# A hybrid decoder layer on one core: weights in long runs, and the mixer without GpSimd

## The chip, the cores and the metric

The kernel runs on one core of a Trainium2 chip. The metric is the device time of one execution, in microseconds. The engines are named as in the profile: PE is TensorE (PEld its weight loads), DVE is VectorE, ACT is ScalarE, POOL is GpSimd, SP is SyncE, which issues all the DMAs.

## What is computed

One layer for 256 tokens of width 1024, all in float32 (DEPTH is 1):

```python
c_act = jax.nn.silu(c)
ada = c_act @ w_ada[l] + b_ada[l]
sh_mix, sc_mix, g_mix, sh_ffn, sc_ffn, g_ffn = jnp.split(ada, N_ADA, axis=-1)
h = modulate(rmsnorm(x, norm_mix[l]), sh_mix, sc_mix)
cols = h @ w_in                       # 11520 columns: lru x, lru gate, q, k, v, rwkv, gates
y_a = rglru_branch(lru_x, lru_gate, ...)       # conv, gates, linear scan
y_b = stick_breaking_attention(q, k, v)        # 8 heads
y_c = rwkv7_branch(rw_cols, ...)               # delta-rule state, 16 heads
merged = g_a * (y_a @ p_lru) + g_b * (y_b @ p_sb) + g_c * (y_c @ p_rwkv)
x = x + g_mix[:, None, :] * (merged @ w_out)
h = modulate(rmsnorm(x, norm_moe[l]), sh_ffn, sc_ffn)
x = x + g_ffn[:, None, :] * moe_ffn(h, ...)    # 32 experts, top 4, clamped SwiGLU
return rmsnorm(x, norm_final)
```

## The kernel before

The work has two halves. The mixer (ada, the three branches, their merge, w_out) multiplies activations that lie transposed in SBUF by weights that are streamed in pieces of 256 columns; the MoE streams all 32 experts' weights, 12 MB each, through a ring of 19 tiles of 1 MB.

A **projection** (`proj`) is 256 columns of a weight matrix against all 256 tokens. `load` fetches it in two halves, tiles `raw` of 128 partitions x 4 x 256 (0.52 MB), through a ring of NRAW = 5 tiles. `split_w` makes two float32r tiles of each half: `whi`, a rounded copy made on ACT, and `wlo`, the rest, a subtraction on DVE or, for every `pool`-th half, on GpSimd (PAT, PLRU, PMG: all halves in the lru branch and the first merge, every second one in the second merge, none in attention). The rings of `whi` and `wlo` are NSP = 3 deep. PE then does 48 matmuls per projection, hi x hi, hi x lo and lo x hi. There are 57 projections and four more products of the same size for w_out.

The **ada** columns come in 24 chunks of 256. The eight that the first norm needs are loaded first, in tiles `raw0` of 1.05 MB, and summed on PE (`ada_cols`: eight matmuls of 32 columns against the silu of c, a copy out of PSUM, two matmuls that turn the row into columns). The other sixteen are taken by `ada_next`. In attention, whose four pairs of heads call it three times each, a chunk goes to GpSimd (`ada_cols_g`): two loads into a ring `araw` of its own, a multiplication and sums on GpSimd, and the last two matmuls (`end`) a call later. In the lru branch the other four go through `load` and `ada_cols`.

GpSimd also has the scaling of `qr` (line 418), two steps of the group norm (573, 574), the convolution's first tap (738) and two products of the lru branch (755, 766).

A scheduler of the framework sets the order of each engine's instructions from a cost model; `sooner(n)` raises the priority of a piece, `tc.issue_after` keeps a load from moving ahead. So the branches interleave: the second half of rwkv, with its **triangular solve** (lines 488 to 493, 31 steps of a multiplication and a subtraction on DVE), runs beside the lru branch. On each engine the order is then fixed, and a waiting instruction holds all behind it. SP's queue holds the loads in the order in which ring slots are expected to come free; each waits for the engine that last read the slot.

`x1`, the norm of the MoE and the first 7 expert tiles take the place of rwkv's buffers when these are done; further ring tiles open as the merge, w_out and the splits end. In the MoE each expert is 64 matmuls for gate and up (line 1081), 32 for down (1108) and the scatter (1123); `ew` (879) loads a tile as soon as its slot is free.

Of the kernel before, what the change touches and what calls it, by code (L numbers as in the profile page):

```python
# [80 lines left out]
def trace(tc, pools, I, out, dbg, stop):  # L81
# [139 lines left out]

    def ada_cols_g(pool, nk, col, dst):

        r = mixer.tile([128, 256], F32, name="adarow", tag="adarow", bufs=2)
        for k in range(0, KT, nk):
            raw = pool.tile([128, nk, 256], F32, name="araw", tag="araw", bufs=2)
            with tc.issue_after(last[0].ins):
                SY.dma_start(raw, ada_src(col)[:, k:k + nk])
            G.tensor_tensor(raw, raw, bcast(csil[:, k:k + nk], 2, 256), ALU.mult)  # L229
            if nk == 4:  # L230
                G.tensor_tensor(raw[:, 0:2], raw[:, 0:2], raw[:, 2:4], ALU.add)
            if k == 0:
                G.tensor_tensor(r, raw[:, 0], raw[:, 1], ALU.add)
            else:
                G.tensor_tensor(r, r, raw[:, 0], ALU.add)
                G.tensor_tensor(r, r, raw[:, 1], ALU.add)

        def end():
            ps = ptp([128, 2], "adacol")
            for i in range(2):  # L240
                T.matmul(ps[:, i:i + 1], r[:, i * 128:i * 128 + 128], onesq[:, 0:1], start=True, stop=True)
            V.tensor_tensor(dst, ps, P("b_ada", col // 128, 2), ALU.add)

        return end
# [1101 lines left out]
```

## Time and profile before

| | |
|---|---|
| median of 3 runs | 1581.53 us (1578.42 to 1583.39) |
| the profiled execution | 1581.08 us, its span 1579.4 us |
| busy in the span | PE 92%, DVE 43%, ACT 25%, POOL 17% |
| DMA | 498.84 MB, 167350 packets; 99921 of them under 2 KB |
| expert weights | 384 loads of 1 MB, all on SP's queue |

The page gives busy time by engine over the whole span; the stretches differ so much that the rows by window say more. A matmul's duration on the page includes its pipeline, so PE's busy share is no measure of how near it is to its peak. A wait is put down to what ended it.

### The profile page before, as it was taken

How to read it: one execution, taken by the hardware profiler on the slowest of the kernel's cores; microseconds unless marked ns; L12 is line 12 of the kernel's file. 1: busy time of each engine (PE TensorE's matmuls, PEld its weight loads, DVE VectorE, ACT ScalarE, POOL GpSimd, SP SyncE). 2: the span in 40 equal slices, each digit the busy share in tenths (PEclk: the TensorE clock that was granted, in tenths of full speed). 3: DMA queues.
4: the chain of work that ended last, by engine and by line, in shares of the span. 5: the costliest groups of instructions: out<-in, count | busy, mean ns of one | idle time of the engine just before them, and what ended most of it. 6: DMA issues, size and time to landing. Idle time of an engine off the chain costs nothing. (4 is left out here: it accounts for less than half of the span.)

```text
span 1579.4 us, 20890 instructions
## 1 busy us (share of the span) xinstructions
PE 1459.9 (92%) x8416; PEld 833.8 (53%) x8416; DVE 686.6 (43%) x1284; ACT 397.1 (25%) x692; POOL 264.5 (17%) x213
## 2 busy tenths in 40 slices
PE   6999799987999998999999889999989989989897
PEld 4889799876899997334333223333323223223233
DVE  5698945889628655222313113313213212212323
ACT  4634333754735443101101001001001001101101
POOL 0184673655544100000000000000000000000000
PEclk7979879988999998999999999999999999999999
DMA  9655543343335968899999999999999999999995
GB/s 324 202 184 162 159 155 101 116 138 111 113 118 155 317 227 321 351 418 417 418 416 418 417 416 416 418 416 417 417 418 415 418 418 415 418 418 416 417 419 204
DMA packets 167350, 498.84 MB, mean 316 GB/s; under 512 B 12625, under 2 KB 99921, under 8 KB 134481
## 3 DMA queue, kind: packets, MB, share of 16 engines
q1 hardware_dynamic: 167248, 497.46, 81.9%
q8 instruction: 68, 1.11, 0.3%
q14 instruction: 34, 0.27, 0.0%
HBM read 496.37 MB, written 1.05 MB: 315 GB/s over the span
## 5 line engine op out<-in xcount | busy, mean ns | idle before, releaser
L1081 PE MATMUL pg<-ew,xe 128*64 128x512 f32 x1024 | 273.7, 612 | 29.0 <-DMA ew<-in_w_gu_dram 28.7
L1081 PE MATMUL pu<-ew,xe 128*64 128x512 f32 x1024 | 264.2, 597 | 0.0
L1108 PE MATMUL pd<-ew,act 128*64 128x512 f32 x992 | 230.4, 601 | 22.8 <-ACT act L1100 22.8
L174 PE MATMUL mm<-hhi,whi 128*128 128x256 f32 x720 | 216.0, 300 | 6.5 <-ACT whi L153 6.5
L174 PE MATMUL mm<-hhi,wlo 128*128 128x256 f32 x720 | 215.6, 300 | 3.3 <-DVE wlo L156 2.8
L174 PE MATMUL mm<-hlo,whi 128*128 128x256 f32 x720 | 216.0, 300 | 0.0
L1081 PEld LDWEIGHTS pg<-ew,xe 128*64 128x64 f32 x1024 | 68.3, 138 | 179.8 <-issue 103.9
L153 ACT ACTIVATE whi<-raw 128x1024 fp32r<-128x1024 f32 x122 | 128.8, 1058 | 123.8 <-PE mm L174 98.8
L174 PEld LDWEIGHTS mm<-hhi,whi 128*128 128x128 f32 x720 | 146.3, 203 | 10.5 <-ACT whi L153 6.7
L1081 PEld LDWEIGHTS pu<-ew,xe 128*64 128x64 f32 x1024 | 74.6, 138 | 146.2 <-issue 146.2
L174 PEld LDWEIGHTS mm<-hhi,wlo 128*128 128x128 f32 x720 | 146.4, 204 | 8.2 <-issue 3.4
L1108 PEld LDWEIGHTS pd<-ew,act 128*64 128x64 f32 x992 | 69.4, 138 | 151.9 <-issue 115.1
L174 PEld LDWEIGHTS mm<-hlo,whi 128*128 128x128 f32 x720 | 146.8, 204 | 5.3 <-issue 4.7
L1114 DVE TENSOR_TENSOR yd<-pd,gff 128x512 f32<-128x512 f32 x31 | 21.5, 692 | 269.2 <-PE pd L1108 244.6
L156 DVE TENSOR_TENSOR wlo<-raw,whi 128x1024 fp32r<-128x1024 f32 x82 | 112.4, 1373 | 51.1 <-ACT whi L153 50.7
L156 POOL TENSOR_TENSOR wlo<-raw,whi 128x1024 fp32r<-128x1024 f32 x40 | 98.7, 2469 | 95.5 <-ACT whi L153 93.5
L1123 PE MATMUL pc<-yd,swt 64*128 64x512 f32 x248 | 96.0, 628 | 0.0
L1125 DVE TENSOR_TENSOR x<-x,pc 128x512 f32<-128x512 f32 x124 | 84.1, 680 | 11.6 <-PE pc L1123 10.7
L1123 PEld LDWEIGHTS pc<-yd,swt 64*128 64x128 f32 x248 | 30.0, 185 | 49.8 <-issue 28.5
L229 POOL TENSOR_TENSOR araw<-araw,csil 128x1024 f32<-128x1024 f32 x24 | 51.0, 2129 | 31.3 <-DMA araw<-in_w_ada_dram 31.3
L1053 ACT ACTIVATE xe<-xps,adaf,A 128x256 f32<-128x256 f32 x32 | 18.1, 565 | 100.4 <-DVE xe L1052 100.1
L1100 ACT ACTIVATE act<-act_ps 128x256 f32<-128x256 f32 x64 | 24.5, 383 | 72.8 <-PE act_ps L1098 71.4
(820 smaller groups left out, 1878.6 us busy)
## 6 DMA issues: line engine op xcount, KB each, us to landing
ew<-in_w_gu_dram SPq DMA_DIRECT2D x256, 1024.0 KB, 20.0
ew<-in_w_down_dram SPq DMA_DIRECT2D x128, 1024.0 KB, 20.0
raw<-in_w_in_dram SPq DMA_DIRECT2D x90, 512.0 KB, 4.3
araw<-in_w_ada_dram SPq DMA_DIRECT2D x24, 512.0 KB, 4.9
raw<-in_w_ada_dram SPq DMA_DIRECT2D x8, 1024.0 KB, 12.4
raw<-in_w_ada_dram SPq DMA_DIRECT2D x8, 512.0 KB, 3.6
raw<-in_p_sb_dram SPq DMA_DIRECT2D x8, 512.0 KB, 3.5
raw<-in_p_lru_dram SPq DMA_DIRECT2D x8, 512.0 KB, 3.5
```

What stands on the lines that cost most here:

```text
L153: A.activation(hi, src, AF.Copy)
L156: eng.tensor_tensor(lo, src, r32(hi), ALU.subtract)
L174: T.matmul(ps[:, c], w[i][:, k, c * 128:c * 128 + 128], x[j][:, q * 4 + k], start=(q + c + k + n == 0), stop=(q == 1 and k == 3 and n == 2 ...
L229: G.tensor_tensor(raw, raw, bcast(csil[:, k:k + nk], 2, 256), ALU.mult)
L1053: A.activation(xe[:, k + 1, 0:n], xps[:, 1, 0:n], AF.Identity, scale=A2[:, k + 1:k + 2], bias=sh2[:, k + 1:k + 2])
L1081: i = T.matmul(p[hf * 64:hf * 64 + 64], xe[:, k], gu[k][:, c0:c0 + 512], start=False, stop=(k == KT - 1), skip_group_check=True)
L1100: A.activation(at, tp, AF.Copy)
L1108: i = T.matmul(pd[hf * 64:hf * 64 + 64], at[:, k % 2, (k // 4) * 64:(k // 4) * 64 + 64], w[:, hf * 512:hf * 512 + 512], start=(n == 0), st ...
L1114: V.tensor_tensor(yd, pd, gff2, ALU.mult)
L1123: T.matmul(ps, swt[sl, t], yd[sl], start=True, stop=True)
L1125: V.tensor_tensor(y[:, t, csl], y[:, t, csl], ps, ALU.add)
```

## The change

The host lays the weights out by pieces. w_ada, w_in, the three branch projections and w_out become arrays [piece of 256 columns, half, partition, 1024], so that a half is one run of 4 KB per partition instead of four of 1 KB; w_down's tiles get one run of 8 KB per partition instead of two of 4 KB (w_gu had such runs). The rwkv up-projections and the b_gu rows are stacked so that one load replaces two and four. Bytes and matmuls stay as they were.

In the mixer GpSimd keeps memsets and masks alone. All low parts go to DVE; the twelve ada chunks of attention go through `load` and `ada_cols` on PE, and the sixteen late chunks leave PSUM on ACT instead of DVE; the two products of the lru branch and the second centring go to DVE; the scaling of `qr`, the squares and the first tap go to ACT. NRAW becomes 7, and the ring `araw` goes.

```diff
-    NRAW, NSP = 5, 3
+    NRAW, NSP = 7, 3
     def ada_src(col):
-        return I["w_ada"].rearrange("(k p) n -> p k n", p=128)[:, :, col:col + 256]
+        return I["w_ada"][col // 256].rearrange("q p n -> p q n")
     def load(src, col):
-        v = src.rearrange("(k p) n -> p k n", p=128)
         for q in range(2):
             t = wraw.tile([128, 4, 256], F32, name="raw", tag="raw", bufs=NRAW)
-            last[0] = SY.dma_start(t, v[:, q * 4:q * 4 + 4, col:col + 256])
+            last[0] = SY.dma_start(t.rearrange("p k n -> p (k n)"), src[col // 256, q])
-    PAT, PLRU, PMG = 0, 1, (1,2,0)
-    def split_w(src, pool=None):
+    def split_w(src):
         A.activation(hi, src, AF.Copy)
-        nsplit[0] += 1
-        eng = G if pool and nsplit[0] % pool == 0 else V
-        eng.tensor_tensor(lo, src, r32(hi), ALU.subtract)
+        V.tensor_tensor(lo, src, r32(hi), ALU.subtract)
-    def ada_cols(raw, col, dst, pspace=ptp):
+    def ada_cols(raw, col, dst, pspace=ptp, late=False):
-        V.tensor_copy(r, ps)
+        if late:
+            A.activation(r, ps, AF.Copy)
+        else:
+            V.tensor_copy(r, ps)
-    def ada_cols_g(pool, nk, col, dst):
...
-            SY.dma_start(raw, ada_src(j * 256))
+            SY.dma_start(raw.rearrange("p (q k) n -> p q (k n)", q=2), ada_src(j * 256))
-        SY.dma_start(upw[0:64], I["rw_w_up"][:, b * 512:b * 512 + 512])
-        SY.dma_start(upw[64:128], I["rw_a_up"][:, b * 512:b * 512 + 512])
+        SY.dma_start(upw, I["rw_up"][b])
-                G.tensor_scalar(qr[:, cl, :, 0:64], ch(kx), P("rw_k_k", ct), None, ALU.mult)
+                A.activation(qr[:, cl, :, 0:64], ch(kx), AF.Copy, scale=P("rw_k_k", ct))
-            (G if t else V).tensor_tensor(yv[:, t], yv[:, t], bcast(mean[:, t], 2, 64), ALU.subtract)
-            G.tensor_tensor(sq[:, t], yv[:, t], yv[:, t], ALU.mult)
+            V.tensor_tensor(yv[:, t], yv[:, t], bcast(mean[:, t], 2, 64), ALU.subtract)
+            A.activation(sq[:, t], yv[:, t], AF.Square)
-    def ada_next(pool=None, nk=4):
-        if ends:
-            ends.pop(0)()
+    def ada_next():
...
-        if pool:
-            ends.append(ada_cols_g(pool, nk, 2048 + i * 256, dst[:, 2 * j:2 * j + 2]))
-        else:
-            ada_cols(load(I["w_ada"], 2048 + i * 256), 2048 + i * 256, dst[:, 2 * j:2 * j + 2])
+        ada_cols(load(I["w_ada"], 2048 + i * 256), 2048 + i * 256, dst[:, 2 * j:2 * j + 2], late=True)
-            G.tensor_scalar(xc, xr[:, cc], P("conv_w", ct), P("conv_b", ct), ALU.mult, ALU.add)
+            A.activation(xc, xr[:, cc], AF.Identity, scale=P("conv_w", ct), bias=P("conv_b", ct))
-        G.tensor_tensor(gt, gq, gt, ALU.mult)
+        V.tensor_tensor(gt, gq, gt, ALU.mult)
-            G.tensor_tensor(ix, s8, ix, ALU.mult)
+            V.tensor_tensor(ix, s8, ix, ALU.mult)
-            for i in range(4):
-                SY.dma_start(raw[i * 32:i * 32 + 32], I["b_gu"][:, j * D + i // 2 * 512:j * D + i // 2 * 512 + 512])
+            SY.dma_start(raw, I["b_gu2"][j])
-    dsrc = I["w_down"].rearrange("e (q k p) n -> e q p k n", p=128, k=2)
+    dsrc = I["w_down"].rearrange("e q p (k n) -> e q p k n", k=2)
+def pieces(w, n, parts):
+    rows, cols = w.shape
+    v = w.reshape(parts, rows // parts // 128, 128, cols // n, n).transpose(3, 0, 2, 1, 4)
+    return np.ascontiguousarray(v).reshape(cols // n, parts, 128, -1)
```

The scheduler makes a new order of this. Three places matter here. Names of tiles carry numbers that differ between the programs.

SP's queue where attention begins, before: halves of w_in go into `raw`, halves of ada chunks into `araw`.

```order
L142 DMA raw_1477<-in_w_in_dram 128x4x256
L142 DMA raw_1479<-in_w_in_dram 128x4x256
L228 DMA araw_1482<-in_w_ada_dram 128x4x256
L228 DMA araw_1487<-in_w_ada_dram 128x4x256
L142 DMA raw_1552<-in_w_in_dram 128x4x256
L142 DMA raw_1554<-in_w_in_dram 128x4x256
L142 DMA raw_1631<-in_w_in_dram 128x4x256
L228 DMA araw_1561<-in_w_ada_dram 128x4x256
```

The same queue after the change, from the second pair's V to the third pair's V, with the engines whose progress each load waits for (DMAHW stands for an earlier DMA, DVE for a split, PE for an ada chunk's matmuls):

```order
L142 DMA raw_2092<-in_w_in_dram 128x1024 [waits DMAHW1_49,DVE_49]
L142 DMA raw_2094<-in_w_in_dram 128x1024 [waits DMAHW4_49,DVE_49]
L142 DMA raw_2096<-in_w_ada_dram 128x1024 [waits DMAHW6_49,DMAHW5_49,DVE_49]
L142 DMA raw_2098<-in_w_ada_dram 128x1024 [waits DMAHW7_49,PE_49]
L142 DMA raw_2174<-in_w_in_dram 128x1024 [waits PE_49]
L142 DMA raw_2176<-in_w_in_dram 128x1024 [waits PE_49]
L142 DMA raw_2178<-in_w_ada_dram 128x1024 [waits DMAHW2_49,PE_49]
L142 DMA raw_2180<-in_w_ada_dram 128x1024 [waits DMAHW3_49,PE_49]
L142 DMA raw_2256<-in_w_in_dram 128x1024 [waits PE_49]
L142 DMA raw_2258<-in_w_in_dram 128x1024 [waits DMAHW0_49,DVE_49]
```

Ada halves now alternate with w_in halves in one ring; the first two rows are the third pair's Q, `raw_2174` and `raw_2176` its K.

PE at that place after the change: the end of the third pair's Q (mm_2116), three ada chunks, and the first matmul of its K (mm_2198).

```order
L194 MATMUL adaps_1792<-raw_1790,crep_92 32x256 x4
L168 MATMUL mm_2116<-hhi_134,wlo_2146 128x256
L168 MATMUL mm_2116<-hhi_134,whi_2145 128x256
L168 MATMUL mm_2116<-hlo_135,whi_2145 128x256
L168 MATMUL mm_2116<-hhi_134,wlo_2146 128x256
L202 MATMUL adacol_1803<-quad_94,adarow_1801 128x1 x2
L194 MATMUL adaps_1874<-raw_1870,crep_92 32x256 x4
L194 MATMUL adaps_1874<-raw_1872,crep_92 32x256 x4
L202 MATMUL adacol_1885<-quad_94,adarow_1883 128x1 x2
L194 MATMUL adaps_1956<-raw_1952,crep_92 32x256 x4
L194 MATMUL adaps_1956<-raw_1954,crep_92 32x256 x4
L168 MATMUL mm_2198<-hhi_134,whi_2199 128x256
```

Before, only the two matmuls of an `adacol` stood here, since GpSimd had made the sums. The three chunks belong to the second pair, and hold their slots up to here.

DVE at the beginning of the second triangular solve, before (`subt` and `xb` are the solve):

```order
L492 TENSOR_TENSOR subt<-lb,xb 128x30
L493 TENSOR_TENSOR xb<-xb,subt 128x30
L492 TENSOR_TENSOR subt<-lb,xb 128x58
L493 TENSOR_TENSOR xb<-xb,subt 128x29x2
L492 TENSOR_TENSOR subt<-lb,xb 128x56
L493 TENSOR_TENSOR xb<-xb,subt 128x28x2
```

And after the change:

```order
L150 TENSOR_TENSOR wlo<-raw,whi 128x1024
L464 TENSOR_TENSOR subt<-lb,xb 128x30
L203 TENSOR_TENSOR adag<-adacol,pc 128x2
L465 TENSOR_TENSOR xb<-xb,subt 128x30
L464 TENSOR_TENSOR subt<-lb,xb 128x58
L465 TENSOR_TENSOR xb<-xb,subt 128x29x2
L727 SCALAR_TENSOR_TENSOR s_3927<-bb,s_3927 128x512
L464 TENSOR_TENSOR subt<-lb,xb 128x56
L465 TENSOR_TENSOR xb<-xb,subt 128x28x2
L150 TENSOR_TENSOR wlo<-raw,whi 128x1024
```

Before, no low part stands inside this solve on DVE, since the lru branch's are on GpSimd; now sixteen and more do. On PE the matmuls that follow the solve (line 505, now 477) stand after 34.2 projections before, and after 39.1 now.

## Rows read from the trace of the kernel before

**Rows 1.** The page: busy time, share of the span and instructions of each engine.

```profile
PE 1459.9 (92%) x8416; PEld 833.8 (53%) x8416; DVE 686.6 (43%) x1284; ACT 397.1 (25%) x692; POOL 264.5 (17%) x213
```

**Rows 2.** Busy us by stretch: length, engines (instructions), granted clock, DMA share, GB/s.

```profile
0.00:52.00 52.00, 38.24 (x290) 28.18 (x291) 27.15 (x85) 24.53 (x37) 4.25 (x32) 0.80 0.99 304
52.00:110.00 58.00, 55.45 (x367) 47.49 (x365) 46.33 (x63) 32.88 (x53) 32.74 (x23) 0.91 0.61 192
110.00:300.00 190.00, 178.97 (x1419) 167.34 (x1420) 141.53 (x226) 78.84 (x122) 107.32 (x94) 0.88 0.45 137
300.00:420.00 120.00, 102.41 (x850) 89.35 (x850) 109.85 (x186) 67.82 (x99) 69.42 (x41) 0.87 0.44 133
420.00:500.00 80.00, 79.37 (x663) 74.96 (x661) 36.62 (x44) 41.29 (x55) 39.41 (x18) 0.98 0.37 109
500.00:600.00 100.00, 97.90 (x784) 93.43 (x785) 66.43 (x91) 45.96 (x67) 11.37 (x6) 1.00 0.80 269
...
660.00:1558.00 898.00, 842.31 (x3666) 293.65 (x3663) 228.39 (x512) 86.21 (x214) 0.00 (x0) 0.98 1.02 416
```

**Rows 3.** PE's longest wait between 660 and 1560: total us, times, longest.

```profile
PE pg L1081 <- DMA ew<-in_w_gu_dram: 28.7, 39, 4.2
```

**Rows 4.** Windows: 4 KB runs of w_down, 8 KB of w_gu, 1 KB of w_ada.

```profile
1308.00:1312.00 4.00, 4.00 (x17) 1.38 (x17) 2.57 (x7) 0.42 (x1) 0.00 (x0) 1.00 1.03 410
1320.00:1326.00 6.00, 5.16 (x27) 2.08 (x26) 1.17 (x2) 1.54 (x4) 0.00 (x0) 1.00 1.01 422
8.00:34.00 26.00, 20.24 (x169) 10.71 (x169) 12.32 (x48) 7.71 (x15) 0.00 (x0) 0.75 1.09 348
```

**Rows 5.** POOL's timeline from 360 us: start, duration, line, operands.

```profile
361.84 2.53 POOL L156 TENSOR_TENSOR wlo<-raw,whi 128x1024 fp32r<-128x1024 f32 x1 [2.75 <-ACT whi L153]
366.39 2.45 POOL L156 TENSOR_TENSOR wlo<-raw,whi 128x1024 fp32r<-128x1024 f32 x1 [2.03 <-ACT whi L153]
```

**Rows 6.** DVE's timeline in the same stretch.

```profile
360.76 0.42 DVE L747 TENSOR_TENSOR ix<-ix,xc 128x256 f32<-128x256 f32 x1
...
362.03 2.61 DVE L747 TENSOR_TENSOR ix<-ix,xc 128x256 f32<-128x256 f32 x1
...
366.64 2.35 DVE L493 TENSOR_TENSOR xb<-xb,subt 128x126 f32<-128x126 f32 x1
...
369.83 0.28 DVE L493 TENSOR_TENSOR xb<-xb,subt 128x120 f32<-128x120 f32 x1
```

**Rows 7.** DVE's groups by form, 300 to 420: busy us, mean ns, idle before.

```profile
L740 DVE SCALAR_TENSOR_TENSOR xc<-xr,pc,xc 128x254 f32<-128x254 f32 x8 | 9.8, 1243 | 0.0
L740 DVE SCALAR_TENSOR_TENSOR xc<-xr,pc,xc 128x255 f32<-128x255 f32 x8 | 8.1, 1026 | 0.0
...
L740 DVE SCALAR_TENSOR_TENSOR xc<-xr,pc,xc 128x253 f32<-128x253 f32 x8 | 3.6, 469 | 0.0
```

**Rows 8.** DVE's groups in 560 to 600, where POOL is idle.

```profile
L156 DVE TENSOR_TENSOR wlo<-raw,whi 128x1024 fp32r<-128x1024 f32 x14 | 17.0, 1222 | 9.7 <-ACT whi L153 9.7
```

**Rows 9.** PE's timeline, 0 to 50: two ada chunks, at full clock and at half.

```profile
15.97 1.07 PE L200 MATMUL adaps<-raw,crep 128*32 128x256 f32 x16
...
21.74 1.93 PE L200 MATMUL adaps<-raw,crep 128*32 128x256 f32 x16 [0.79 <-DMA raw<-in_w_ada_dram]
```

**Rows 10.** Waits of SP's queue, 52 to 500: total us, times, longest.

```profile
SPq L142 <- POOL wlo L156: 137.4, 31, 9.5
...
SPq L228 <- POOL adarow L233: 26.5, 5, 6.9
```

**Rows 11.** DMA issues by line: count, size, median us from issue to landing.

```profile
raw<-in_p_sb_dram SPq DMA_DIRECT2D x8, 512.0 KB, 3.5
```

**Rows 12.** The page's costliest groups: ACT's high parts.

```profile
L153 ACT ACTIVATE whi<-raw 128x1024 fp32r<-128x1024 f32 x122 | 128.8, 1058 | 123.8 <-PE mm L174 98.8
```

**Rows 13.** Tile wlo in 300 to 500: durations min/median/max, first and last start.

```profile
L156 POOL TENSOR_TENSOR wlo<-raw,whi x34: 2349/2402/2773, 301.6 to 497.3; 128x1024 fp32r<-128x1024 f32 x34
```

More of the change, by code (lines that the diff above doesn't have):

```diff
@@ L164, in pmm, with proj @@
         return psum.tile([128, 512], F32, name=name, tag="mm", bufs=3)
-    def proj(raw, x, pool=None):
+    def proj(raw, x):
         ps = pmm().rearrange("p (c t) -> p c t", c=2)
         for q in range(2):
-            w = split_w(raw[q], pool)
+            w = split_w(raw[q])
             for c in range(2):
@@ L220, in ada_cols_v @@
         V.tensor_tensor(dst, ps, P("b_ada", col // 128, 2), ALU.add)
-    def ada_cols_g(pool, nk, col, dst):
[L224 to L233, printed above, removed]
-            else:
[L235 to L244, printed above, removed]
     def diag2(t, cols):
@@ L370, in rwkv_half @@
         upw = rw.tile([128, 512], F32, name="upw")
-        SY.dma_start(upw[0:64], I["rw_w_up"][:, b * 512:b * 512 + 512])
-        SY.dma_start(upw[64:128], I["rw_a_up"][:, b * 512:b * 512 + 512])
+        SY.dma_start(upw, I["rw_up"][b])
         gup = rw.tile([128, 512], F32, name="gup")
-        SY.dma_start(gup, I["rw_g_up"][:, b * 512:b * 512 + 512])
+        SY.dma_start(gup, I["rw_g_up"][b])
         qr = rw.tile([128, 4, 4, 128], F32, name="qr")
@@ L616, in trace @@
     later = list(range(16))
-    ends = []
-    def ada_next(pool=None, nk=4):
-        if ends:
-            ends.pop(0)()
+    def ada_next():
         if not later:
@@ L626, in ada_next @@
         dst, j = ((adag, i) if i < 4 else (adaf, i - 4) if i < 12 else (adag, i - 8))
-        if pool:
-            ends.append(ada_cols_g(pool, nk, 2048 + i * 256, dst[:, 2 * j:2 * j + 2]))
-        else:
-            ada_cols(load(I["w_ada"], 2048 + i * 256), 2048 + i * 256, dst[:, 2 * j:2 * j + 2])
+        ada_cols(load(I["w_ada"], 2048 + i * 256), 2048 + i * 256, dst[:, 2 * j:2 * j + 2], late=True)
     ap = pools("attn", bufs=1)
@@ L689, in attention_pair @@
             if ADA[pr][i]:
-                ada_next(ap)
+                ada_next()
             t = a2("qkv")
-            ps = proj(raw, h2, PAT)
+            ps = proj(raw, h2)
             A.activation(t, ps, AF.Copy, scale=128.0 ** -0.5 if i == 0 else 1.0)
@@ L724, in lru_pair @@
         raw_x, raw_g = load(w_in, OFF_LX + b * 256), load(w_in, OFF_LG + b * 256)
-        if ends:
-            ends.pop(0)()
         if ADAL[b]:
@@ L729, in lru_pair @@
         xr = l2("xr")
-        A.activation(xr, proj(raw_x, h2, PLRU), AF.Copy)
+        A.activation(xr, proj(raw_x, h2), AF.Copy)
         for cc in range(2):
@@ L747, in lru_pair @@
             V.tensor_tensor(ix[:, cc], ix[:, cc], xc, ALU.mult)
-        ps = proj(raw_g, h2, PLRU)
+        ps = proj(raw_g, h2)
         gq = g2("gq")
@@ L915, in trace @@
             sg = g2("gsig")
-            A.activation(sg, proj(raw_g, h2, PMG[br]), AF.Sigmoid)
-            ps = proj(raw_p, yhl, PMG[br])
+            A.activation(sg, proj(raw_g, h2), AF.Sigmoid)
+            ps = proj(raw_p, yhl)
             if br == 0:
@@ L1319, in trace, with halves @@
         finish(gain(ew_tile()[:, 0:D]))
+def pieces(w, n, parts):
+    rows, cols = w.shape
+    v = w.reshape(parts, rows // parts // 128, 128, cols // n, n).transpose(3, 0, 2, 1, 4)
+    return np.ascontiguousarray(v).reshape(cols // n, parts, 128, -1)
+def halves(w):
+    return np.ascontiguousarray(w.reshape(w.shape[0], 2, -1).transpose(1, 0, 2))
 def layout(x, c, w_ada, b_ada, norm_mix, norm_moe, norm_final, w_in, conv_w, conv_b,
@@ L1328, in layout @@
     res = {"x": a["x"][0], "pc": np.ascontiguousarray(pc), "b_router": a["b_router"]}
-    for n in ("w_ada", "w_in", "rw_w_up", "rw_a_up", "rw_g_up", "p_lru", "p_sb", "p_rwkv",
-              "w_out", "w_router", "w_gu", "b_gu", "w_down", "b_down"):
+    for n in ("p_lru", "p_sb", "p_rwkv", "w_out", "w_in", "w_ada"):
+        res[n] = pieces(a[n][0], 256, 2)
+    res["w_down"] = np.ascontiguousarray(a["w_down"][0].reshape(NE, 4, 2, 128, D).transpose(0, 1, 3, 2, 4)).reshape(NE, 4, 128, 2 * D)
+    for n in ("w_router", "w_gu", "b_gu", "b_down"):
         res[n] = a[n][0]
+    res["rw_up"] = halves(np.concatenate([a["rw_w_up"][0], a["rw_a_up"][0]]))
+    res["rw_g_up"] = halves(a["rw_g_up"][0])
+    b = a["b_gu"][0].reshape(NE, 2, 2, 512).transpose(1, 2, 0, 3)
+    res["b_gu2"] = np.ascontiguousarray(np.stack([b, b], axis=2)).reshape(2, 128, 512)
     res["lru_w"] = np.stack([a["lru_wa"][0], a["lru_wx"][0]], axis=2)
```

1 line of the change is left out of this document (removed).

## The prediction

> **What bounds the kernel now.** I read first the page's busy line [rows 1], then the span cut into stretches [rows 2], then the waits inside a stretch. The profiled execution took 1581.08 us, 1579.4 of it span; the median of the runs shown is 1581.53, so the sum below, made against 1581.08, can be read against either. A measurement of this kernel can tell about 0.3%, 4.7 us, from no change.
>
> Rows 2 show two kernels in one. From 660 us to 1558 us the DMA share is 1.02 at 416 GB/s: the expert weights stream without a pause, and TensorE, 842.3 us busy of 898, waits for them [rows 3]. What counts there is bytes per us, and when the stream gets going. Before that, the mixer is no single engine's. In 300 to 420 VectorE is busy 109.9 of 120 us while TensorE is idle for 17.6, with a granted clock of 0.87; in 110 to 300 TensorE is idle for 11.0 us, at 0.88; from 420 on TensorE is nearly full at a clock of 0.98 to 1.00. The DMA share of 0.37 to 0.61 between 52 and 500 says that bandwidth is not what the mixer lacks.
>
> Part of VectorE's busy time is not work. At 361.84 GpSimd starts a low part of 2.53 us [rows 5]; a VectorE multiplication of two SBUF tiles that takes 0.42 us at 360.76 takes 2.61 at 362.03, and ends as GpSimd ends. The same happens to the triangular solve at 366.64 (2.35 instead of 0.28) [rows 6]. The convolution taps with 253 columns take 469 ns and the same taps with 254 columns 1243 [rows 7]: (1243 - 469) x 8 = 6.2 us, and (1026 - 469) x 8 = 4.5 us, lost in two groups alone. SyncE pays too: it stands 137.4 us for GpSimd's low parts and 26.5 us for its ada sums, with weight loads queued behind [rows 10].
>
> **The change, term by term.**
>
> *Long runs at the start.* The eight ada chunks of 1.049 MB come in 1 KB runs at 348 GB/s in 8 to 34 us; in the stream, 4 KB runs move at 410 [rows 4]. 8.39 MB take 24.1 us at the one and 20.5 at the other: **-3.6 us**, on the path, because the first projection waits for the last chunk. The single load of the small rw and b_gu tables instead of two and four only shortens SyncE's queue; nothing is counted.
>
> *Long runs in the stream.* The gate-up weights already come in 8 KB runs; w_down goes from 4 KB to 8 KB: 410 against 422 GB/s [rows 4]. 898 us at 416 GB/s are 373.6 MB, a third of it w_down: 124.5 MB take 303.7 us or 295.1: **-8.6 us**. Between nothing and this lies the range; I take the end, as TensorE has 56 us of room in the stretch [rows 2].
> The Trainium skill speaks against both terms: "DMA: Bandwidth & Descriptors", Specifications, puts line rate at transfers of 512 B and more, so 1 KB runs would already be enough, and gives 358 GB/s as HBM's limit for a core. By that both terms would be 0. The trace disagrees on both: 348, 410 and 422 by length, and 416 sustained.
>
> *Ada on TensorE.* Twelve chunks move from GpSimd. A chunk's eight matmuls take 1.07 us at full clock and 1.93 at half [rows 9]: 12 x 1.07 = **+12.8 us** (23.2 at half clock) in 110 to 300, where TensorE is 94% busy. Their sums to columns were on TensorE before. Sixteen copies out of PSUM, eight scalings, eight convolution starts and four squares go to ScalarE; none can exceed the 1.058 us of a split four to eight times as wide [rows 12], so 38 us at the very most, and ScalarE has 25 to 112 us free in each of these stretches [rows 2]: nothing.
>
> *The ring that ada now shares.* This is the term of the order rows. Twelve chunks now take slots of the seven-slot ring, two each, and TensorE works off three in a row at a pair's end. SyncE's rows show what follows: the two halves of the next K weights wait for PE, that is for the chunk's matmuls. Each then needs its turn behind one other half (0.52 MB at 410: 1.3 us), a landing of 3.5 us [rows 11], and a split of 1.06 on ScalarE and 1.22 on VectorE [rows 8, 12]: 7.1 us. TensorE has two more chunks, their columns and four matmuls meanwhile, some 3.2 us. So 3.9 us of waiting; I charge it at two of the four groups, **+7.8 us**. The lower end is 0 (loads early enough), the upper is the first rival.
>
> *VectorE without GpSimd.* In 52 to 110 TensorE loses 2.6 us idle and 0.09 x 58 = 5.2 to the clock; in 110 to 300, 11.0 and 0.12 x 190 = 22.8; in 300 to 500, 18.2 and 0.13 x 120 + 0.02 x 80 = 17.2 [rows 2]. I expect the idle time back, and half of the clock's, since the clock fell where the engine had been waiting: **-5.2, -22.4 and -26.8 us**. Ends: nothing, and all of it.
> Against that, VectorE takes over 34 low parts between 300 and 500 [rows 13], 34 x 1.222 = 41.5 us [rows 8], and eight products of 512 columns, between 0.42 and 1.22 us each, say 0.7: 47 us. What it gets back there lies between 10.7 us (the two groups above) and GpSimd's whole 108.8 us [rows 2]; I take 40. VectorE ends 7 us longer in a stretch where it is nearly full: **+7 us**. The order rows show that the second solve now stretches over split after split, so part of that lands where VectorE had 43 us free, in 420 to 500.
>
> From 500 to 660 and in the last 21 us I expect nothing: TensorE is 98% busy there, or the code is the same.
>
> Sum: -3.6 - 8.6 + 12.8 + 7.8 - 5.2 - 22.4 - 26.8 + 7 = -39.0 us; 1581.1 - 39 = **1542 us**. By the start and the stream alone, nothing would remain after the ada matmuls are paid.
>
> **The rivals.**
>
> *The shared ring starves TensorE (slower).* Three held chunks are six of seven slots. If all twelve chunks make TensorE wait for a load and a split, 7.1 us less one chunk's own 1.07 each, that is 12 x 6.0 = 72 us in place of 7.8: 1542 - 7.8 + 72 = 1606. It decides from (39.0 + 7.8) / 12 = 3.9 us per chunk. For it: the order rows name PE in SyncE's waits six times in a row. Against it: splits run up to three halves ahead (NSP), and TensorE has a projection's remaining matmuls to work on wherever a group does not stand right at a projection's end. 9%.
>
> *The stalls are hidden anyway (no change).* TensorE counts 94% busy in 110 to 300. If VectorE's lost time only fills gaps that other waits would leave, the start and the stream bring 12.2 us and the ada matmuls cost 12.8: 1582. For it: in 110 to 300 TensorE is idle for only 6% of the time. Against it: GpSimd's blocking falls in the solve, which everything behind it in the rwkv branch needs. 7%.
>
> *Everything comes back (faster still).* All idle time and all lost clock of 52 to 500, 31.8 + 45.2 us, plus 12.2, less 12.8: 1581.1 - 76.4 = 1505. 20%.
>
> *Runs of 1 KB are long enough already.* Then 12.2 us fall away: 1554. The page named above would have it so. The rates of rows 4 contradict it, though they stand beside other differences of place: 4%.
>
> **The numbers.** The forecast has 60%. Faster by more than 0.3% (under 1577) are the forecast, the third and the fourth rival and a little of the second: 0.85. Within 0.3%: most of the second, 0.05. Slower: the first and the rest of the second, 0.10. The range runs from 1508, close to the third rival, to 1577; outside lie the first rival, most of the second and some of the third, about 2 in 10.
>
> **What would show it.** Right: no VectorE product over 1 us in the solve; DMA near 400 GB/s in the first 30 us, and the first projection 3 to 4 us sooner; 420 GB/s in the stream, its last byte about 39 us sooner; the second solve longer than before on the clock, with TensorE busy throughout. Wrong: TensorE gaps of 4 us and more after each group of three ada chunks; a stretch of 300 to 500 no shorter, with VectorE full; a stream that TensorE bounds, its DMA share under 1.

## The result and the profile after

The changed kernel takes 1555.92 us (median of 4 runs, 1551.51 to 1559.59) against 1580.68 of before in the same comparison: a ratio of 0.9841, 95% interval 0.9809 to 0.9873. It is faster, by 24.8 us where 39 were forecast. A second comparison gave 1554.19 and 0.9852 (0.9821 to 0.9883). The profiled execution took 1559.59 us, 1557.8 of it span: 21.6 less than the profiled one of before.

The page's busy line, in the columns of [rows 1]:

```profile
PE 1455.1 (93%) x8608; PEld 830.7 (53%) x8608; DVE 643.3 (41%) x1330; ACT 413.3 (27%) x728; POOL 11.0 (1%) x59
```

GpSimd has 11.0 us of work left for 264.5, and VectorE is 43 us less busy though it has 40 low parts more. The span by stretch, in the columns of [rows 2]:

```profile
0.00:52.00 52.00, 39.89 (x322) 30.20 (x323) 30.49 (x92) 28.81 (x45) 4.25 (x32) 0.90 0.88 341
52.00:110.00 58.00, 58.00 (x463) 49.32 (x462) 41.13 (x73) 34.50 (x55) 1.41 (x4) 1.00 0.52 170
110.00:300.00 190.00, 179.03 (x1465) 159.82 (x1465) 107.63 (x216) 80.76 (x129) 2.31 (x18) 0.89 0.42 141
300.00:420.00 120.00, 110.29 (x877) 101.70 (x877) 105.02 (x218) 89.86 (x134) 1.20 (x3) 0.94 0.47 155
420.00:500.00 80.00, 80.00 (x753) 75.32 (x752) 38.57 (x45) 29.09 (x40) 0.00 (x0) 0.96 0.34 110
500.00:600.00 100.00, 99.78 (x807) 95.15 (x805) 69.07 (x112) 48.71 (x78) 1.80 (x2) 1.00 0.78 297
660.00:1534.00 874.00, 820.39 (x3593) 287.52 (x3590) 223.12 (x500) 84.99 (x211) 0.00 (x0) 0.99 1.01 420
```

The row to look at is 110 to 300: VectorE is 34 us less busy there, and yet TensorE is idle for 11.0 us and at 0.89 of its clock, as before (11.0 and 0.88). 52 to 110 is now full at full clock.

The mixer from its first projection matmul to the last one of w_out, before and after (same columns):

```profile
34.72:612.69 577.97, 544.07 (x4298) 501.90 (x4299) 418.38 (x640) 280.50 (x415) 263.25 (x201) 0.92 0.54 171
```

```profile
30.99:597.66 566.67, 545.99 (x4491) 499.12 (x4492) 374.57 (x686) 296.28 (x451) 9.74 (x47) 0.94 0.51 175
```

So it begins 3.7 us sooner and is 11.3 us shorter. One profile says this only to some us: in the profiled execution of the second comparison (run after_again, the same kernel) the mixer is 5 us shorter again, and its stretch of 110 to 300 has as much idle time (10.7 us) at a clock of 0.92 for 0.89:

```profile
30.49:592.20 561.71, 539.03 (x4489) 493.08 (x4490) 374.95 (x686) 296.00 (x451) 10.69 (x47) 0.95 0.51 177
110.00:300.00 190.00, 179.28 (x1507) 160.57 (x1504) 111.72 (x225) 84.94 (x137) 2.31 (x18) 0.92 0.43 144
```

The rates, in the windows of [rows 4] (w_down, w_gu, the first ada chunks):

```profile
1308.00:1312.00 4.00, 4.00 (x22) 1.29 (x18) 0.00 (x0) 0.00 (x0) 0.00 (x0) 1.00 1.01 420
1320.00:1326.00 6.00, 5.47 (x23) 1.96 (x22) 4.57 (x11) 1.19 (x3) 0.00 (x0) 1.00 1.02 423
8.00:34.00 26.00, 21.89 (x186) 13.66 (x187) 15.92 (x54) 10.05 (x17) 0.00 (x0) 0.83 1.03 409
```

(The first two windows stand at places of the stream; all its runs are 8 KB now.) The stream moves 420 GB/s where it moved 416, the start 409 where it moved 348.

VectorE's groups in 300 to 420, which answer to [rows 7], and the multiplications of both triangular solves (tile `subt`: shortest, median and longest ns, first and last start):

```profile
L150 DVE TENSOR_TENSOR wlo<-raw,whi 128x1024 fp32r<-128x1024 f32 x28 | 34.2, 1221 | 4.9 <-ACT whi L149 4.6
...
L703 DVE SCALAR_TENSOR_TENSOR xc<-xr,pc,xc 128x255 f32<-128x255 f32 x8 | 3.8, 480 | 0.0
L703 DVE SCALAR_TENSOR_TENSOR xc<-xr,pc,xc 128x254 f32<-128x254 f32 x8 | 3.7, 478 | 0.0
L703 DVE SCALAR_TENSOR_TENSOR xc<-xr,pc,xc 128x253 f32<-128x253 f32 x8 | 3.7, 479 | 0.0
...
L464 DVE TENSOR_TENSOR subt<-lb,xb x62: 176/263/301, 126.5 to 418.3; 128x126 f32<-128x126 f32 x6, 128x30 f32<-128x30 f32 x4, 128x56 f32<-128x56 f32 x4, 128x78 f32<-128x78 f32 x4
```

The taps of 1243 and 1026 ns are all 480 now, and no multiplication of the solve takes over 0.301 us, where before the longest took 2.358. The stalls of VectorE beside GpSimd, the mechanism behind [rows 5, 6], are gone. The Trainium skill ("SBUF — State Buffer", SBUF: two separate sides) says that an operation of VectorE with two SBUF inputs and one of GpSimd that reads SBUF take a shared pair of ports for a whole instruction in turn. The trace of before agrees: in [rows 5, 6] the two long operations of VectorE end 0.27 and 0.15 us after the low parts of GpSimd beside which they started.

What TensorE waits for in 110 to 420, before and after, the longest lines of each list (total us, times, longest):

```profile
PE mm L174 <- ACT whi L153: 6.5, 1, 6.5
PE tp L744 <- issue: 5.7, 1, 5.7
PE tp L675 <- DVE beta L672: 4.8, 2, 3.2
PE tp L744 <- DVE xc L740: 2.9, 1, 2.9
PE mm L174 <- DVE wlo L156: 2.8, 2, 1.7
```

```profile
PE mm L168 <- ACT gsig L878: 6.7, 1, 6.7
PE ssq L389 <- ACT k_sq L388: 4.3, 1, 4.3
PE mm L168 <- ACT gq L714: 3.0, 1, 3.0
PE mm L168 <- ACT whi L149: 2.4, 2, 1.6
```

By the whole lists VectorE ended 11.7 us of these waits before and 2.6 after, ScalarE 8.8 before and 18.1 after: ScalarE has taken VectorE's place. Its timeline before the longest of these waits ends (start, duration):

```profile
398.35 1.06 ACT L149 ACTIVATE whi<-raw 128x1024 fp32r<-128x1024 f32 x1
399.43 1.28 ACT L722 ACT_TABLE_LOAD   x1
400.72 0.63 ACT L722 ACTIVATE aa<-s 128x512 f32<-128x512 f32 x1
401.38 0.63 ACT L723 ACTIVATE s<-s 128x512 f32<-128x512 f32 x1
401.92 0.61 ACT L726 ACTIVATE bb<-aa 128x512 f32<-128x512 f32 x1
402.55 1.28 ACT L878 ACT_TABLE_LOAD   x1
403.85 0.60 ACT L878 ACTIVATE gsig<-mm 128x512 f32<-128x512 f32 x1
```

TensorE needs the PSUM tile that the sigmoid of line 878 is to empty, and the sigmoid stands behind the lru branch's last steps and two table loads.

### The profile page after: what moved, and what is told of

Same layout as the page of the kernel before. It is cut to its first block, busy times and chain, and to the rows that moved or that the text cites. A ratio compares the mean times of both kernels' runs of the same rounds, so it can differ in the third digit from the quotient of the medians.

```text
span 1557.8 us, 21164 instructions
## 1 busy us (share of the span) xinstructions
PE 1455.1 (93%) x8608; PEld 830.7 (53%) x8608; DVE 643.3 (41%) x1330; ACT 413.3 (27%) x728; POOL 11.0 (1%) x59
## 5 line engine op out<-in xcount | busy, mean ns | idle before, releaser
L1043 PE MATMUL pg<-ew,xe 128*64 128x512 f32 x1024 | 269.4, 603 | 25.2 <-DMA ew<-in_w_gu_dram 25.2
L168 PE MATMUL mm<-hhi,whi 128*128 128x256 f32 x720 | 212.6, 295 | 5.7 <-ACT gq L714 3.0
L168 PE MATMUL mm<-hhi,wlo 128*128 128x256 f32 x720 | 211.2, 293 | 1.1 <-DVE wlo L150 1.1
L168 PE MATMUL mm<-hlo,whi 128*128 128x256 f32 x720 | 211.7, 294 | 0.0
L150 DVE TENSOR_TENSOR wlo<-raw,whi 128x1024 fp32r<-128x1024 f32 x122 | 148.9, 1223 | 96.4 <-ACT whi L149 95.3
L168 PEld LDWEIGHTS mm<-hhi,whi 128*128 128x128 f32 x720 | 142.5, 198 | 12.8 <-issue 3.8
L168 PEld LDWEIGHTS mm<-hhi,wlo 128*128 128x128 f32 x720 | 142.2, 197 | 7.8 <-issue 5.2
L168 PEld LDWEIGHTS mm<-hlo,whi 128*128 128x128 f32 x720 | 142.3, 198 | 5.6 <-issue 4.8
L1076 DVE TENSOR_TENSOR yd<-pd,gff 128x512 f32<-128x512 f32 x31 | 21.5, 692 | 270.8 <-PE pd L1070 246.2
L1087 DVE TENSOR_TENSOR x<-x,pc 128x512 f32<-128x512 f32 x124 | 84.4, 683 | 11.7 <-PE pc L1085 10.7
L1015 ACT ACTIVATE xe<-xps,adaf,A 128x256 f32<-128x256 f32 x32 | 18.1, 565 | 101.3 <-DVE xe L1014 101.0
L194 PE MATMUL adaps<-raw,crep 128*32 128x256 f32 x384 | 30.3, 433 | 9.9 <-DVE spt L579 9.1
L1014 DVE TENSOR_SCALAR xe<-xps,A,adaf 128x256 f32<-128x256 f32 x32 | 17.4, 544 | 44.4 <-PE xps L1011 44.4
## 6 DMA issues: line engine op xcount, KB each, us to landing
ew<-in_w_gu_dram SPq DMA_DIRECT2D x256, 1024.0 KB, 19.8
ew<-in_w_down_dram SPq DMA_DIRECT2D x128, 1024.0 KB, 19.8
```

The costliest lines, as they stand in the source:

```text
L150: V.tensor_tensor(lo, src, r32(hi), ALU.subtract)
L168: T.matmul(ps[:, c], w[i][:, k, c * 128:c * 128 + 128], x[j][:, q * 4 + k], start=(q + c + k + n == 0), stop=(q == 1 and k == 3 and n == 2 ...
L194: T.matmul(ps[32 * j:32 * j + 32], crep[:, q * 4 + j, :], raw[q][:, j], start=(q == 0), stop=(q == 1))
L1014: V.tensor_scalar(xe[:, k, 0:n], xps[:, 0, 0:n], A2[:, k:k + 1], sh2[:, k:k + 1], ALU.mult, ALU.add)
L1015: A.activation(xe[:, k + 1, 0:n], xps[:, 1, 0:n], AF.Identity, scale=A2[:, k + 1:k + 2], bias=sh2[:, k + 1:k + 2])
L1043: i = T.matmul(p[hf * 64:hf * 64 + 64], xe[:, k], gu[k][:, c0:c0 + 512], start=False, stop=(k == KT - 1), skip_group_check=True)
```

## The experiments

All times in one table. Five comparisons stand behind it: the changed kernel's first; runs_only to low_gpsimd; the changed kernel's second with no_ada, own_ring and mix_c; ada_load to ring_eight; and ada_late. The kernel before had medians of 1576.89 to 1580.99 in them, so across comparisons the ratios compare best (0.001 is 1.6 us).

| kernel | median us | ratio to before | 95% interval |
|---|---|---|---|
| changed kernel, first and second time | 1555.92, 1554.19 | 0.9841, 0.9852 | 0.9809-0.9873, 0.9821-0.9883 |
| runs_only | 1564.15 | 0.9911 | 0.9879-0.9942 |
| mixer_only | 1572.83 | 0.9971 | 0.9954-0.9988 |
| ada_gpsimd | 1559.42 | 0.9875 | 0.9843-0.9908 |
| low_gpsimd | 1572.20 | 0.9976 | 0.9946-1.0006 |
| no_ada | 1524.94 | 0.9666 | 0.9650-0.9682 |
| own_ring | 1556.65 | 0.9865 | 0.9848-0.9881 |
| mix_c | 1556.96 | 0.9868 | 0.9850-0.9885 |
| ada_load | 1535.98 | 0.9730 | 0.9694-0.9767 |
| psum_by_dve | 1563.07 | 0.9885 | 0.9846-0.9925 |
| ring_eight | 1551.09 | 0.9830 | 0.9791-0.9870 |
| ada_late | 1545.94 | 0.9772 | 0.9750-0.9794 |

**The two halves of the change.** runs_only takes the new layout and its loads into the kernel before; mixer_only takes the old ones into the changed kernel:

```diff
 runs_only, against before
-            last[0] = SY.dma_start(t, v[:, q * 4:q * 4 + 4, col:col + 256])
+            last[0] = SY.dma_start(t.rearrange("p k n -> p (k n)"), src[col // 256, q])
 ...
 mixer_only, against the changed kernel
-            last[0] = SY.dma_start(t.rearrange("p k n -> p (k n)"), src[col // 256, q])
+            last[0] = SY.dma_start(t, v[:, q * 4:q * 4 + 4, col:col + 256])
 ...
```

> The kernel before with the long runs alone: its mixer keeps GpSimd, five ring slots and ada's own tiles. Theory (the parts add up): 4 us sooner at the first projection, the stream 9 us shorter (890 us from 373 MB left to 2 MB left becomes 881), the mixer's 578 us from projection 0 to 61 as before: 1581 - 13 = 1568. Rival (the mixer takes the start's gain back, because its pace is set by VectorE and GpSimd): 1572. Rival (the stream's gain needs the other mixer): 1577.

> The changed mixer (no GpSimd, ring of seven) with the short runs of before. Theory (the parts add up): only the mixer's 11 us: 1570, stream at 416 GB/s. Rival (the mixer gains nothing by itself, all of it is runs): 1581. Rival (1 KB runs starve the shared ring, its loads land later): 1585 or more.

> The changed kernel itself, timed again beside the other three, so that parts can be compared on one chip: ratio to the kernel before 0.984, as in the first comparison. If instead it comes out near 0.988, the parts runs_only (0.991) and mixer_only (0.997) simply add up; if it stays at 0.984, the two parts together bring some 7 us more than apart.

The long runs alone bring 13.0 us, as their theory said. The mixer alone brings 4.4, less than the 11 that the profile gives it; on top of the layout it brings 9 to 11, by the ratios (0.9911 to 0.9852 and 0.9841). The two ratios make 0.9882 together, just above the one interval of the changed kernel (0.9873) and at the end of the other (0.9883): whether the halves bring a few us more together than apart these runs don't settle. Either way the larger half of the gain is the layout. The first 8 to 34 us and the stream, in runs_only and then in mixer_only (the columns of the windows), show that the rates go with the layout:

```profile
8.00:34.00 26.00, 21.91 (x186) 13.53 (x187) 15.93 (x54) 9.77 (x17) 0.00 (x0) 0.83 1.03 408
660.00:1530.00 870.00, 819.40 (x3586) 287.10 (x3587) 222.23 (x499) 83.51 (x209) 0.00 (x0) 0.99 1.01 421
```

```profile
8.00:34.00 26.00, 20.43 (x170) 11.25 (x170) 12.53 (x48) 7.43 (x15) 0.00 (x0) 0.72 1.09 348
660.00:1530.00 870.00, 813.00 (x3545) 284.23 (x3543) 219.56 (x492) 83.10 (x208) 0.00 (x0) 0.98 1.02 417
```

**The two moves within the mixer.** ada_gpsimd gives the twelve chunks back to GpSimd, with the old sums, two tiles of their own and a ring of five; low_gpsimd gives back the low parts:

```diff
 ada_gpsimd
-                ada_next()
+                ada_next(ap)
 ...
 low_gpsimd
-        V.tensor_tensor(lo, src, r32(hi), ALU.subtract)
+        eng = G if pool and nsplit[0] % pool == 0 else V
+        eng.tensor_tensor(lo, src, r32(hi), ALU.subtract)
 ...
```

> The changed kernel with its twelve late ada chunks put back on GpSimd (ring of five, two tiles of ada's own), all low parts staying on VectorE. Theory A (idle time and lost clock of 110 to 300 did not come down, so the move of ada paid 12.8 us on TensorE for nothing): 1556 - 13 = 1543. Theory B (GpSimd's sums block VectorE, which costs about what the ada matmuls cost): 1556. Theory C (blocking costs all that I had forecast for the stretch, 22 us, less 12.8): 1566.

> The changed kernel with the 40 low parts of the lru branch and the gates put back on GpSimd, ada staying on TensorE. Theory (the 15 us less idle time and lost clock between 300 and 500 come from here): 1556 + 15 = 1571, products of 2 us and more on VectorE again. Rival (VectorE is so full there that taking the low parts over costs what it frees): 1556. Rival (the ACT table loads of the stretch set the pace): 1556 as well, but with TensorE waiting on ScalarE.

For ada the time is nearest to theory B's: with 1559.4 against 1554 to 1556 the move of ada is worth some 3 to 5 us, which the intervals can't tell from nothing. That GpSimd's sums hold VectorE up, as B has it, shows in the multiplications of the solve (tile `subt`) in ada_gpsimd, which take up to 1.87 us again.

For the low parts the theory holds: undoing their move costs 16 to 18 us by the medians, 20 to 21 by the ratios. The waits of low_gpsimd's TensorE between 300 and 420, and a tap of VectorE there:

```profile
PE tp L712 <- issue: 9.2, 2, 6.1
PE tp L712 <- DVE xc L708: 6.4, 1, 6.4
...
L708 DVE SCALAR_TENSOR_TENSOR xc<-xr,pc,xc 128x254 f32<-128x254 f32 x8 | 9.9, 1256 | 0.0
```

A tap of 1256 ns is back (1243 before), and TensorE stands 15.6 us before line 712's matmuls, which read what the taps make; for 6.4 of these the profile names the taps, for 9.2 it names nothing. Together with runs_only the two make a square, all with long runs: both kinds of work on GpSimd 1564.2, ada moved 1572.2, low parts moved 1559.4, both moved 1554 to 1556. The first corner, runs_only, differs from the others in one thing more, the small operations that it keeps on GpSimd and VectorE; they have no run of their own. So moving ada with these operations (and with it the ring), the low parts still on GpSimd, is a loss of 8 us, while with the low parts moved ada's move is no loss. Each move seems worth more once the other is made; why, these runs don't show.

**What ada costs.** no_ada leaves the twelve chunks out, ada_load loads them only:

```diff
 no_ada
+        if i < 12:
+            V.tensor_copy(dst[:, 2 * j:2 * j + 2], P("b_ada", 16 + i * 2, 2))
 ...
 ada_load
+        raw = load(I["w_ada"], 2048 + i * 256)
+        if i < 12:
+            for q in range(2):
+                V.tensor_copy(dst[:, 2 * j + q:2 * j + q + 1], raw[q][:, 0, 0:1])
 ...
```

> The changed kernel without its twelve late ada chunks in the attention pairs: neither loaded nor multiplied, their columns hold the bias alone. Theory (the move of ada costs TensorE its matmuls and little more): 1556 - 13 = 1543. Theory (the shared ring's waits and the half clock behind them, 18 us between 140 and 200, are ada's too): 1556 - 13 - 18 = 1525. Rival (the stretch is bound elsewhere, by the solve and ScalarE): 1553.

> As no_ada, but the twelve chunks are loaded into the shared ring as in the changed kernel, and VectorE reads one column of each half (their columns of the output are wrong): slots and transfers are kept, TensorE's matmuls, the column matmuls and ScalarE's copies are gone. Theory (TensorE's own work makes the price: 12 x 1.07 matmuls and 12 x 0.6 columns are 20 of the 29 us, the rest follows from it): 1527, close to no_ada. Rival (the loads and the slots make the 9 us that are left): 1535. Rival (most of the price is loads and slots): 1540 or more.

The twelve chunks cost 1554.2 - 1524.9 = 29.3 us on TensorE, and 1559.4 - 1524.9 = 34.5 on GpSimd (33 by the ratios). The 1525 of no_ada's second theory came, but own_ring, below, does not bear out its mechanism, the waits of the ring. Of the 29.3, 11.0 are loads and what waits behind them (ada_load against no_ada; 10 by the ratios, uncertain by some 6). In ada_load VectorE's read frees a slot and not TensorE's matmuls, so what the longer holding of slots costs is not in the 11.0 but in the rest, 18.3, with TensorE's work and the copies. TensorE's groups in the changed kernel, 90 to 300 us:

```profile
L194 PE MATMUL adaps<-raw,crep 128*32 128x256 f32 x192 | 14.3, 406 | 0.0
L202 PE MATMUL adacol<-quad,adarow 128*128 128x1 f32 x48 | 7.2, 253 | 0.5 <-ACT adarow L197 0.5
```

14.3 us for the chunks (12.8 forecast), and 7.2 for the columns, which TensorE had before too: 21.5 us of busy time in all. The first rival of ada_load, 1535, is what came.

**The shared ring.** own_ring gives ada two tiles and the rest five; ring_eight has one slot more; mix_c puts ada by place on TensorE (before the first solve, and in the lru branch) and on GpSimd (behind it):

```diff
 own_ring
-    NRAW, NSP = 7, 3
+    NRAW, NSP = 5, 3
 ...
-            t = wraw.tile([128, 4, 256], F32, name="raw", tag="raw", bufs=NRAW)
+            n = "araw" if own else "raw"
+            t = wraw.tile([128, 4, 256], F32, name=n, tag=n, bufs=2 if own else NRAW)
 ...
 ring_eight
-    NRAW, NSP = 7, 3
+    NRAW, NSP = 8, 3
 mix_c (on ada_gpsimd; 1 is TensorE, 2 GpSimd)
-    ADA = ((1, 1, 1),) * 4
+    ADA = ((1, 1, 1), (1, 0, 0), (2, 2, 2), (2, 2, 2))
-    ADAL = (1, 1, 1, 1)
+    ADAL = (2, 2, 1, 1)
```

> The changed kernel with its ada halves in two tiles of their own and the other weights in a ring of five: the same memory, but no weight waits for an ada matmul. Theory (shared ring is what starves TensorE between 140 and 200): up to 18 us less, 1538, no gap behind the ada chunks. Rival (five slots are too few once ada takes DMA turns and SyncE stands for ada's own two tiles): 1556 or more. The chunks also spread out in TensorE's order, from threes to ones and twos.

> Ada split by place: chunks of the first solve's stretch on TensorE (four) or put off into the lru branch (three more), the six chunks behind the first solve on GpSimd, with a ring of five. Theory (GpSimd's sums cost nothing where VectorE has no solve and is half idle, 200 to 280): TensorE saves 6 x 1.07 = 6.4 us, and part of the waits of 140 to 200 go: 1556 - 12 = 1544. Rival (the five slots, or chunks in the lru branch where ScalarE is full, take it back): 1556.

> The changed kernel with eight ring slots in place of seven. Theory (own_ring showed that the gaps behind the ada chunks go without any gain, so the ring is not what bounds): 1555, within 4 us. Rival (one slot more ends the wait for K's weights and the half clock behind it): 1540 to 1550.

The changed kernel from 140 to 300, and own_ring in the same stretch (the columns of the windows):

```profile
140.00:160.00 20.00, 16.24 (x117) 13.46 (x118) 14.61 (x48) 5.57 (x9) 0.13 (x2) 0.78 0.58 211
160.00:180.00 20.00, 19.46 (x202) 18.41 (x202) 12.46 (x14) 7.62 (x12) 0.13 (x2) 0.67 0.27 85
180.00:200.00 20.00, 20.00 (x158) 16.57 (x157) 5.83 (x11) 6.91 (x12) 0.13 (x2) 0.84 0.34 113
200.00:300.00 100.00, 93.92 (x743) 83.22 (x741) 52.22 (x98) 48.03 (x77) 1.78 (x10) 0.94 0.43 145
```

```profile
140.00:160.00 20.00, 20.00 (x182) 17.61 (x181) 17.53 (x50) 7.59 (x11) 0.13 (x2) 1.00 0.73 257
160.00:180.00 20.00, 20.00 (x241) 18.32 (x240) 12.90 (x14) 7.37 (x11) 0.13 (x2) 0.83 0.39 133
180.00:200.00 20.00, 20.00 (x136) 18.06 (x134) 4.46 (x9) 6.74 (x13) 0.13 (x2) 0.74 0.09 27
200.00:300.00 100.00, 91.57 (x681) 74.02 (x680) 50.91 (x99) 46.26 (x77) 1.78 (x10) 0.91 0.43 141
```

With ada's own ring TensorE isn't idle at all from 140 to 200, where the changed kernel has 4.3 us of idle time, and the time of the whole is the same. Part of what it gained is lost at once: from 200 to 300 it is idle for 8.4 us where the changed kernel is for 6.1, at 0.91 of the clock for 0.94. So the waits behind the ada chunks are real, and ending them in this way only moves the waits on. The theory's 1538 falls; but own_ring also takes two slots from the other weights, so its rival, that five are too few, isn't excluded. The theory of mix_c falls too (1557.0 for 1544), with a ring of five as well. ring_eight, which gives a slot and takes none, comes out at 1551.1, which can't be told from the changed kernel.

**ScalarE's waits.** psum_by_dve lets VectorE empty the PSUM tiles on which TensorE waited at 385 and 397:

```diff
-        A.activation(gt, ps, AF.Copy)
-        A.activation(gq, ps, AF.Square, scale=math.sqrt(0.044715))
+        V.tensor_copy(gt, ps)
+        A.activation(gq, gt, AF.Square, scale=math.sqrt(0.044715))
...
-            A.activation(sg, proj(raw_g, h2), AF.Sigmoid)
+            ps = proj(raw_g, h2)
+            if br == 0 and pr < 2:
+                V.tensor_copy(sg, ps)
+                ps = sg
+            A.activation(sg, ps, AF.Sigmoid)
```

> The changed kernel, but VectorE empties the PSUM tile of each lru gate projection (ScalarE squares the copy) and those of the first two merge gates (ScalarE's sigmoid reads the copy), so that TensorE does not wait for ScalarE's table loads at 385 and 397. Theory (these two waits, 9.7 us, and the half clock behind them, 5 to 7 us, are why 300 to 420 gave back only a part): 1555 - 10 to 1555 - 16 = 1539 to 1545. Rival (VectorE, 105 of 120 us busy there, is late with six more copies of 0.7 us): 1555 or slower.

The theory missed: 1563.1, if anything slower, as the rival said. TensorE's waits from 300 to 420:

```profile
PE mm L168 <- DVE gsig L880: 4.3, 1, 4.3
PE mm L168 <- DVE gt L713: 3.9, 1, 3.9
```

VectorE's queue is about as late as ScalarE's: 8.2 us where ScalarE made it 9.7. In the changed kernel VectorE is busy for 105 of these 120 us, ScalarE for 90.

**A faster version.** ada_late moves the chunks into the first two merges, with eight slots:

```diff
-    ADA = ((1, 1, 1),) * 4
+    ADA = ((0, 0, 0),) * 4
+    ADAG = ((2, 2, 2, 2), (1, 1, 1, 1), (0, 0, 0, 0))
...
             raw_g, raw_p = load(w_in, gcol + pr * 256), load(I[pw], pr * 256)
+            for _ in range(ADAG[br][pr]):
+                ada_next()
```

(The line that makes A2 of ada's columns moves behind them.)

> The changed kernel with eight ring slots and its twelve late ada chunks moved once more, still on TensorE: out of the attention pairs and into the first two merges (two for each of four steps, then one for each of four), where TensorE is full at nearly full clock and the DMA share is 0.3 to 0.4. Theory (ada_load minus no_ada: 11 us of ada's price are loads, slots and the waits behind them in the attention stretch; the 20 us of matmuls and columns stay): 1551 - 9 to 1555 - 11, some 1543. Rival (the loads now collide with the second solve's stretch, where ScalarE and VectorE are full, or with the first expert weights): 1551 or slower.

1545.9 us and 0.9772: faster than the changed kernel, whose intervals begin above this one's end, and 36 us faster than before by the ratio. Its 110 to 300, and its mixer as a whole:

```profile
110.00:300.00 190.00, 183.37 (x1516) 167.11 (x1516) 133.83 (x264) 101.21 (x160) 3.77 (x21) 0.94 0.34 112
```

```profile
31.09:582.70 551.61, 538.98 (x4490) 493.24 (x4491) 373.13 (x686) 295.46 (x453) 10.21 (x51) 0.95 0.51 179
```

With ada out of attention the stretch has 6.6 us idle and a clock of 0.94; the price of the chunks falls from 29.3 to 1545.9 - 1524.9 = 21.0 us by the medians of two comparisons, or 17 by their ratios (0.9772 and 0.9666). That is the size of TensorE's work for them (14.3 + 7.2). The eighth slot's own share isn't separated: against ring_eight the move gives 5 us by the medians and 9 by the ratios, and these two intervals overlap.

## Why the prediction was right, and where it fell short

The time, 1556, lies in the range of 1508 to 1577 and on the forecast side, 14 us above the 1542. Most of the shortfall is in one place. The table is made from the profiled executions of the first comparison.

| term | forecast | measured |
|---|---|---|
| start | -3.6 | -3.7 (first projection at 30.99 for 34.72) |
| stream | -8.6 | -8.5 (373.6 MB at 420 for 416 GB/s) |
| mixer: ada, ring, stretches, low parts | -26.8 | -11.3 |
| all else | 0 | +1.9 |
| sum, profiled executions | -39.0 | -21.6 |

**Start and stream: right.** Their 12.2 us answer to the 13.0 of runs_only, though its profile has a mixer 3.9 us shorter besides (574.1 us), which no term foresaw and which is within what one profile differs from the next. With 348 against 409 GB/s at the start and 416 against 420 in the stream, in runs_only too, the rival of 1554 (runs of 1 KB are long enough) falls as a mechanism, although its time nearly came: it would have left runs_only at the time of before. The Trainium skill's rule ("DMA: Bandwidth & Descriptors", Specifications) of line rate from 512 B on doesn't hold for these loads.

**Ada's matmuls: +14.3 for +12.8.** The forecast took each chunk at full clock, 1.07 us; one ran at half (1.93), and one in two pieces (1.68 together).

**The ring: right that waits come, wrong that they decide.** The wait for K's weights behind the first three chunks is there, on TensorE's timeline of the changed kernel:

```profile
152.10 1.07 PE L194 MATMUL adaps<-raw,crep 128*32 128x256 f32 x16
154.74 0.58 PE L168 MATMUL mm<-hhi,whi 128*128 128x256 f32 x1 [1.57 <-ACT whi L149]
```

(The landing of 3.5 us in that term was the one of p_sb's halves; the halves of w_in, K's among them, took 4.3 on the same page.) The wait is 1.6 us long, and all waits for high parts in 110 to 420 make 2.4 us, where I had charged 3.9 at two places, 7.8; own_ring took such gaps away without a gain. That this term was too large brought the forecast some 5 us nearer to the result: luck, not insight. The rival of 1606 turned slower only from 3.9 us lost per chunk; ada_load's 11.0 us over twelve chunks make 0.9.

**VectorE without GpSimd: the stalls went, the time came back only in part. This is the step that failed**, and in it the sentence "I expect the idle time back, and half of the clock's" for 110 to 300. Idle time and (1 - clock) x length, from the windows:

| stretch | forecast, with ring and low parts | measured |
|---|---|---|
| 52 to 110 | -5.2 | -2.6 idle, -5.2 clock = -7.8 |
| 110 to 300 | -22.4 + 7.8 = -14.6 | 0 idle, -1.9 clock = -1.9 |
| 300 to 500 | -26.8 + 7 = -19.8 | -8.5 idle, -6.8 clock = -15.3 |

These make -25.0 instead of -39.6; the stretches don't hold quite the same work in both kernels, so single cells are rough, but with ada's +14.3 they make -10.7, and the mixer is 11.3 shorter. Of the 14.6 us missing, 12.7 are in 110 to 300. In the profile of after_again 5.7 of these are back as clock (0.92 for 0.89), and 6.7 of 8.6 missing us are in this stretch. So the size varies with the clock from execution to execution; what does not vary is the idle time, 11.0 and 10.7 us for 11.0.

There the solve is indeed no longer blocked, but that stretch got ada instead, and its other waits filled the room. By the lists of waits in 110 to 300 VectorE ended 8.8 of the 11 us before and 2.6 after, ScalarE 2.3 and 8.4: 4.3 us for k_sq, behind splits and a table load on ScalarE, 2.4 for high parts, 1.2 for `at`. The clock stays at 0.67 to 0.84 between 160 and 200; this comes behind 3.8 us of idle time, but own_ring has 0.83 and 0.74 there without any, so the cause is open. I had treated TensorE's idle time as VectorE's stalls seen from the other side; it was the latest of several waits, and the next came soon after it. That ada loads this stretch is shown from three sides: without the chunks 29.3 us go, loading alone costs some 11, and chunks that run elsewhere cost only 17 to 21. That the move paid no more than some 5 us (ada_gpsimd) agrees. Which wait would have to go next for the stretch to get shorter, beside ada, no run shows.

**300 to 500** came closer. The low parts do cost VectorE what was said (1221 ns each), the second solve stretches from 356 to 418 where it took 355 to 400, and TensorE has no wait behind it between 300 and 500. But TensorE isn't busy throughout: the 9.7 us for ScalarE's gsig and gq, its only waits there, were not on my list, which had costed the operations moved to ScalarE at nothing because it had free time in each stretch. These waits don't show that the moved operations cost anything: none of them stands among the rows ahead of gsig above, and up to 660 us ScalarE loads 32 tables in both kernels. The order has changed, though: 15 of these loads now fall between 300 and 420, where 11 did. Free time in a stretch isn't free time at the moment when a PSUM tile is to be emptied. psum_by_dve shows that it isn't ScalarE alone.

The rival "hidden anyway" (1582) is out as a whole by low_gpsimd, since 16 to 21 us hang on the low parts. In 110 to 300 its mechanism is what came, as the lists of waits have it: there the stalls had covered gaps that other waits now leave. "Everything comes back" (1505) fell with the same step. The last 1.9 us, behind the stream, were not followed up.

## What to carry to other kernels

The stalls that a trace shows are not yet the time that their removal brings: look for the wait that ends next in the same stretch, before counting idle time and lost clock as won. Work moved off a slow engine can cost more than its own duration, here 29 us for 21.5 of TensorE's time; where the engine that takes it was full and fed anyway the same work cost 17 to 21 (with one ring slot more). And test a mixed change by halves: here the plain half, the layout, carried most of the gain.
